# A transformer block on one core: position bias loaded as runs of 219 elements per query column and spread on GpSimd, and shift1/scale1 weights read from an array laid out by chunk

## The chip, the cores and the metric

The kernel runs on 1 core of one Trainium2 chip, in float32. The metric is the device time of one execution in microseconds (us). Three runs of the kernel before took 1788.45, 1788.52 and 1789.22 us; the median is 1788.52.

## The reference

One block of a diffusion transformer is computed for a sequence of 256 tokens (a grid of 4 rows by 64 columns) with 2048 features, beside a context of 256 tokens. Cut to what matters here:

```python
mod = split(silu(c) @ w_mod + b_mod, 6)          # shift1, scale1, gate1, shift2, scale2, gate2
h  = rms_norm(x, norm1_w) * (1 + sc1) + sh1      # hc: the same of ctx, with silu(c_ctx)
q, k, v, ft, pool, sv, sb, sc = split(h @ w_in)  # of hc only k and v
branches = (neighbourhood_attention(q, k, v, kc, vc, rpb), fourier, pooling, short convolution)
y = sum(sigmoid(h @ w_gate[i]) * (branches[i] @ w_branch[i]))
x = x + g1 * (y @ w_o)
x = x + g2 * ((silu(h2 @ w_ffn_gate) * (h2 @ w_ffn_up)) @ w_ffn_down)
```

In the attention each of 8 heads lets a query see, in each of the 4 rows, a window of 16 columns around its own column, and all of the context. To the score of a query in row r and column j with a key in row a and column c the bias `rpb[head, a - r + 7, c - j + 15]` is added; `rpb` has 15 x 31 numbers a head. Keys outside the window of columns are left out.

## The kernel before, in words

**Matrix products.** Each float32 weight tile (128 partitions x 1024, 512 KB) is loaded by the SP queue, rounded by ScalarE into a high part (line 90) and subtracted by VectorE into a low part (line 91), the *split*; TensorE then makes three products, high-high, high-low and low-high (lines 95 to 97). `gemm` does this for the large products, from five raw buffers (`NRAW`): `gt` is w_gate, `br` a branch weight, `wo` w_o, `fg`, `fu` and `dn` the three FFN weights. `in_groups` does the same for w_in, in six chunks of input features (`CHUNKS`, 1, 1, 2, 4, 4 and 4 tiles of 128 features); its sums are `in_x` for the tokens and `in_c` for the context.

**shift1 and scale1.** Before chunk i+1 is multiplied, `prep` makes its modulation and its normed input: `mod1(kt0, nk)` multiplies silu(c) and silu(c_ctx) by the columns of w_mod that belong to nk feature tiles, in four parts of four row tiles each. A part loads its rows of w_mod into tiles called `mod_w` (`mod_tile`, five buffers) and makes four matmuls of 32 columns (line 227, sums `mod_ps`); the fifth step, `finish`, transposes and sums them into modA and modB. `make_h` then transposes the normed tokens (`h_tpx`, `h_tpc`) and applies modA and modB. The steps of `prep` are dealt out between the tiles of the chunk before. Only the first chunk has nothing before it: `mod1(0, 1)` is the program's first work on TensorE. For chunks of one tile a `mod_w` tile has rows of 128 floats (512 bytes), for the others 256 floats (1 KB), always two loads a tile, one for shift and one for scale. The later four modulations (macc, line 405) are summed on VectorE from tiles called `mod`, paced by `pump`.

**Position bias.** Heads come in pairs (h0 = 0, 2, 4, 6). `bias_load(h0)` makes eight loads on GpSimd's own queue: for each head and each of the 4 grid rows of queries, 64 partitions (one a query column; queries stand in reversed column order, so that the source moves by one float from partition to partition) x 4 key rows x 64 floats. `bias_mask(h0)` adds the mask of columns, 0 or -1e30, on GpSimd (line 510). `scores` adds the result to the scores in PSUM on VectorE (line 550).

**Order.** The steps of the four heads' pairs, the norms of q and k and the other branches are functions in a list (`steps`), of which `gemm` and `in_groups` take one at a time; `Bi` are the bias loads, `Ma` the masks, `Sc` the scores. The framework places instructions on the engines by their dependencies and the program's order, and a tile whose buffer is free may be loaded earlier than its step stands. Each engine then works in order. A factor such as `rsh_q` (line 262, a power on GpSimd) belongs to the norm of q.

The few lines that set where the bias steps stand:

```python
steps += [Bi[0], Sq[0], Sq[1], Fa[0], Sq[2], Fa[1], Mu[0], Fa[2], Mu[1], Mu[2]]
steps += [Ma[0], Op[0], Bi[1], Sc[0], Sq[3], No[0], Op[1], Tu[0], Sc[1], Va[0], No[1], Fa[3], Tu[1], Ma[1]]
steps += [Bi[2], Mu[4], Fa[5], Va[3], Mu[5], Ma[2], Op[4], Bi[3], Sc[4], Op[5], No[4], Sc[5], Tu[4],
          No[5], Va[4], Ma[3], Op[6], Tu[5], Sc[6], ...]
```

Of the kernel before, what the change touches and what calls it, by code (L numbers as in the profile page):

```python
# [8 lines left out]
F32 = mybir.dt.float32  # L9
F32R = mybir.dt.float32r  # L10
AF = mybir.ActivationFunctionType
ALU = mybir.AluOpType
# [3 lines left out]
P = 128  # L16
D = 2048
S = 256
NT = S // P
KT = D // P  # L20
INW = 5632
FF = 5632
NH = 8
GRID_W = 64
ROWS = S // GRID_W
EPS = 1e-6
LOAD_AT = 8
# [8 lines left out]
CHUNKS = (1, 1, 2, 4, 4, 4)  # L36
# [6 lines left out]
def block_kernel(ctx: ExitStack, tc: tile.TileContext, t_in, out):  # L43
    nc = tc.nc
    x_d, ctx_d = t_in["x"], t_in["ctx"]
    w_mod, w_in = t_in["w_mod"], t_in["w_in"]
# [4 lines left out]
    sm = ctx.enter_context(tc.tile_pool(name="sm", bufs=1))  # L51
# [3 lines left out]
    def U(name, dtype=F32):  # L55
        return up.tile([P, 1024], dtype, tag="u", name=name, bufs=NU)

    def half(name, dtype=F32):
        return sm.tile([P, 512], dtype, tag="half", name=name, bufs=4)
# [4 lines left out]
    def tr_ps(name):  # L64
        return pst.tile([P, 512], F32, tag="tr", name=name)
# [5 lines left out]
    def mod_tile(name):  # L71
        return wp.tile([P, 1024], F32, tag="mraw", name=name, bufs=NMRAW)
# [132 lines left out]
    def mod1(kt0, nk):  # L205

        nf = nk * P
        box = {}

        def part(k0):  # L210
            if k0 == 0:
                box["ps"] = tr_ps(f"mod1_ps{kt0}")
            ps = box["ps"]
            kn = 2 if nk == 2 else 4
            rvs = []
            for ka in range(k0, k0 + 4, kn):
                raw = mod_tile(f"mod1_w{kt0}_{ka}")
                rv = raw.rearrange("p (k s f) -> p k s f", k=kn, s=2)
                for s_ in range(2):
                    nc.sync.dma_start(  # L220
                        rv[:, :, s_, :],
                        w_mod[ka * P:(ka + kn) * P, s_ * D + kt0 * P:s_ * D + kt0 * P + nf]
                        .rearrange("(k p) f -> p k f", p=P))
                rvs.append(rv)
            for j in range(4):
                kk = k0 + j
                nc.tensor.matmul(  # L227
                    ps[32 * j:32 * j + 32, :2 * nf],
                    lhsT=cst[:, kk, :],
                    rhs=rvs[j // kn][:, j % kn, :, :].rearrange("p s f -> p (s f)"),  # L230
                    start=k0 == 0, stop=k0 == KT - 4)

        def finish():
            ps = box["ps"]
            msb = half(f"msb{kt0}")
            nc.vector.tensor_copy(msb[:, :2 * nf], ps[:, :2 * nf])
            pt_ = tr_ps(f"mod1_t{kt0}")
            for i in range(2 * nk):
                nc.tensor.transpose(pt_[:, i * P:(i + 1) * P], msb[:, i * P:(i + 1) * P], ident)
            red = sm.tile([P, 2, nk, 2], F32, tag=f"red{nk}", name=f"red{kt0}", bufs=2)  # L240
            nc.vector.tensor_reduce(
                red.rearrange("p s k r -> p (s k) r"),
                pt_[:, :2 * nf].rearrange("p (i j r) -> p i r j", j=4, r=32)[:, :, 0:2, :],
                AX.X, ALU.add)
            for s_ in range(2):
                nc.vector.tensor_tensor(
                    red[:, s_], red[:, s_],
                    colB[:, s_ * KT + kt0:s_ * KT + kt0 + nk].unsqueeze(2).to_broadcast([P, nk, 2]),
                    ALU.add)
            nc.vector.tensor_copy(modB[:, kt0:kt0 + nk, :], red[:, 0])  # L250
            nc.vector.scalar_tensor_tensor(
                modA[:, kt0:kt0 + nk, :], red[:, 1], 1.0,
                colA[:, R_N1 + kt0:R_N1 + kt0 + nk].unsqueeze(2).to_broadcast([P, nk, 2]),
                ALU.add, ALU.mult)

        return [lambda k0=k0: part(k0) for k0 in range(0, KT, 4)] + [finish]


# [229 lines left out]
    rpb = t_in["rpb"]  # L488
    wmask = const.tile([P, GRID_W], F32, name="wmask")
    nc.gpsimd.dma_start(wmask, t_in["wmask"])  # L490

    biases = {}

    def bias_load(h0):


        b = U(f"bias{h0}").rearrange("p (h t f) -> p h t f", h=2, t=NT)
        for i in range(2):
            for r in range(ROWS):
                src = bass.AP(rpb.tensor, rpb.offset + (h0 + i) * 15 * 31 + (7 - r) * 31 - 48,  # L500
                              [[1, GRID_W], [31, ROWS], [1, GRID_W]])
                p0 = (r % 2) * GRID_W
                nc.gpsimd.dma_start(
                    b[p0:p0 + GRID_W, i, r // 2, :].rearrange("p (a c) -> p a c", a=ROWS), src)
            biases[h0 + i] = b[:, i]

    def bias_mask(h0):
        for h in (h0, h0 + 1):
            bv = biases[h].rearrange("p t (a c) -> p (t a) c", a=ROWS)
            nc.gpsimd.tensor_tensor(  # L510
                bv, bv, wmask.unsqueeze(1).to_broadcast([P, NT * ROWS, GRID_W]), ALU.add)

    def reverse(v):

# [246 lines left out]
    for i in range(1, len(CHUNKS) - 1):  # L761
        nk = CHUNKS[i]
# [12 lines left out]
    def last(g):  # L775
# [6 lines left out]
    Sq, Fa, Mu = zip(*[qk_norm(lambda st=st, g=g: st[g], n_) for n_, st, g in (  # L782
        ("q0", xin, 0), ("k0", xin, 2), ("c0", cin, 2), ("q1", xin, 1), ("k1", xin, 3), ("c1", cin, 3))])
    Bi, Ma = [[lambda f=f, h=h: f(h) for h in (0, 2, 4, 6)] for f in (bias_load, bias_mask)]

    def nop():
# [114 lines left out]
    for n in range(FF // 512):  # L901
# [11 lines left out]
        for pr in range(2):  # L913
            ps = tr_ps(f"m_tp{n}{pr}")
            for j in range(2):
                for t in range(NT):
                    b = pr * 2 + j
# [80 lines left out]
```

## Time and profile before

| What | Value |
|---|---|
| median of 3 runs | 1788.52 us |
| the profiled execution | 1794.19 us, its span 1792.4 us |
| TensorE busy | 1747.7 us (98%) |
| VectorE, ScalarE, GpSimd busy | 1132.5, 743.8 and 67.9 us |
| granted TensorE clock, mean | 0.992 |
| read from HBM | 400.58 MB, 225 GB/s over the span |

The span runs from the first to the last instruction of the profiled execution; all times of the trace are counted from its start. A busy TensorE is not TensorE at its peak: matmuls are pipelined and their ends modelled, and the granted clock says at what share of full speed they run. The DMA share of a stretch can pass 1, since packets overlap. SP, GpSimd and ScalarE issue loads to the same 16 DMA engines; "to landing" is the time from issue until the data is there.

### The profile page before, as it was taken

The page shows a single profiled execution, that of the slowest core. Times are in us where ns is not written, and L with a number is a line of the kernel's source. Part 1 is how long each engine was busy: PE and PEld are TensorE (multiplying, and loading weights), DVE is VectorE, ACT ScalarE, POOL GpSimd, SP SyncE. Part 2 cuts the span into 40 slices and gives each one's busy share as a digit, 9 for nine tenths or more (in the row PEclk, how much of TensorE's full clock was granted, in tenths as well). Part 3 has the DMA queues.
Part 4 walks back from the last instruction along what each step waited for, and adds up shares of the span by engine and source line. Part 5 has one row for each costly group of instructions (what it writes and reads, how often), then busy time and mean ns, then how long its engine had stood idle before and what let it go on. Part 6 is the DMA issues. An engine that isn't in the chain of part 4 may idle for free.

```text
span 1792.4 us, 21012 instructions
## 1 busy us (share of the span) xinstructions
PE 1747.7 (98%) x7874; PEld 1400.0 (78%) x7874; DVE 1132.5 (63%) x1294; ACT 743.8 (41%) x874; POOL 67.9 (4%) x90
## 2 busy tenths in 40 slices
PE   6998999999997999999999999999999999999998
PEld 3675777887886778888888878888888888888887
DVE  5874564775585876878787877775444444454544
ACT  5322232434553554444444454444444444433342
POOL 0001000031003000000000000000000000000000
PEclk9998999999999999999999999999999999999999
DMA  9788675565569768898999848886666666666663
GB/s 319 249 280 194 194 243 177 163 119 157 166 207 207 244 220 277 292 302 302 320 323 309 290 153 303 305 273 181 191 190 188 188 189 188 190 201 197 208 202 116
DMA packets 212874, 404.08 MB, mean 225 GB/s; under 512 B 14178, under 2 KB 53012, under 8 KB 212772
## 3 DMA queue, kind: packets, MB, share of 16 engines
q1 hardware_dynamic: 209732, 396.37, 68.7%
q0 software_dynamic: 1888, 4.26, 2.8%
q10 hardware_dynamic: 1152, 2.10, 0.3%
q8 instruction: 62, 1.02, 0.2%
q14 instruction: 40, 0.33, 0.1%
HBM read 400.58 MB, written 2.10 MB: 225 GB/s over the span
## 4 chain that ended last, share of the span: by engine, by line
PE 93%; DMA 4%; DVE 1%; issue 1%; SPq 1%; ACT 0%; POOL 0%; POOLq 0%; ACTq 0%; DVEq 0%
PE gt_ps L96 6%; PE gt_ps L97 6%; PE gt_ps L95 6%; PE in_psx L95 5%; PE fu_ps L95 4%; PE fu_ps L96 4%; PE fu_ps L97 4%; PE in_psx L96 4%; PE dn_ps L95 4%; PE dn_ps L97 4%; PE dn_ps L96 4%; PE fg_ps L95 4%; PE fg_ps L97 4%; PE fg_ps L96 4%; PE in_psx L97 4%; DMA gt_w<-in_w_gate 2%
## 5 line engine op out<-in xcount | busy, mean ns | idle before, releaser
L405 DVE SCALAR_TENSOR_TENSOR macc<-mod,cs,macc 128x1024 f32<-128x1024 f32 x128 | 163.3, 1278 | 0.0
L319 DVE TENSOR_TENSOR in_x<-in_x,in_psx 128x512 f32<-128x512 f32 x110 | 74.2, 683 | 47.3 <-PE in_psx L97 47.0
L90 ACT CAST in_2h<-in_w 128x1024 fp32r<-128x1024 f32 x33 | 34.8, 1054 | 165.0 <-PE in_psc L97 96.4
L90 ACT CAST in_0h<-in_w 128x1024 fp32r<-128x1024 f32 (+1 forms) x56 | 57.7, 1034 | 82.9 <-PE in_psc L97 27.0
L95 PE MATMUL in_psx<-in_0h,hxh 128*128 128x512 f32 x220 | 90.5, 418 | 1.3 <-ACT hxh L299 1.0
L96 PE MATMUL in_psx<-in_0l,hxh 128*128 128x512 f32 x220 | 87.8, 402 | 0.0
L97 PE MATMUL in_psx<-in_0h,hxl 128*128 128x512 f32 x220 | 86.4, 395 | 0.0
L91 DVE TENSOR_TENSOR in_0l<-in_w,in_0h 128x1024 fp32r<-128x1024 f32 (+1 forms) x56 | 67.1, 1199 | 10.7 <-ACT in_0h L90 10.7
L91 DVE TENSOR_TENSOR in_2l<-in_w,in_2h 128x1024 fp32r<-128x1024 f32 x33 | 40.4, 1224 | 40.1 <-ACT in_2h L90 40.1
L95 PEld LDWEIGHTS in_psx<-in_0h,hxh 128*128 128x128 f32 x220 | 41.8, 192 | 25.9 <-issue 8.6
L227 PE MATMUL mod_ps<-mod_w,cst 128*32 128x512 f32 (+1 forms) x288 | 46.1, 607 | 11.2 <-DMA mod_w<-in_w_mod 11.2
L96 PE MATMUL in_psx<-in_2l,hxh 128*128 128x512 f32 x132 | 51.8, 392 | 0.0
L95 PE MATMUL in_psx<-in_2h,hxh 128*128 128x512 f32 x132 | 51.5, 390 | 0.0
L97 PE MATMUL in_psx<-in_2h,hxl 128*128 128x512 f32 x132 | 51.5, 390 | 0.0
L96 PEld LDWEIGHTS in_psx<-in_0l,hxh 128*128 128x128 f32 x220 | 42.4, 193 | 10.8 <-issue 1.9
L97 PEld LDWEIGHTS in_psx<-in_0h,hxl 128*128 128x128 f32 x220 | 42.1, 191 | 9.1
L319 DVE TENSOR_TENSOR in_c<-in_c,in_psc 128x512 f32<-128x512 f32 x40 | 27.2, 684 | 28.6 <-PE in_psc L97 28.6
L227 PEld LDWEIGHTS mod_ps<-mod_w,cst 128*32 128x32 f32 x288 | 8.5, 114 | 34.1 <-issue 22.5
L95 PE MATMUL gt_ps<-gt_2h,hxh 128*128 128x512 f32 x64 | 26.6, 420 | 7.9 <-ACT gt_2h L90 7.9
L91 DVE TENSOR_TENSOR gt_2l<-gt_w,gt_2h 128x1024 fp32r<-128x1024 f32 x16 | 19.6, 1224 | 22.7 <-ACT gt_2h L90 22.7
L91 DVE TENSOR_TENSOR gt_12l<-gt_w,gt_12h 128x1024 fp32r<-128x1024 f32 x16 | 20.5, 1282 | 19.9 <-ACT gt_12h L90 19.8
L95 PE MATMUL in_psc<-in_0h,hch 128*128 128x512 f32 x80 | 31.5, 396 | 0.0
(657 smaller groups left out, 5184.4 us busy)
## 6 DMA issues: line engine op xcount, KB each, us to landing
mod<-in_w_mod SPq DMA_DIRECT2D x128, 512.0 KB, 5.5
gt_w<-in_w_gate SPq DMA_DIRECT2D x128, 512.0 KB, 5.5
fg_w<-in_w_ffn_gate SPq DMA_DIRECT2D x88, 512.0 KB, 4.2
fu_w<-in_w_ffn_up SPq DMA_DIRECT2D x88, 512.0 KB, 3.8
dn_w<-in_w_ffn_down SPq DMA_DIRECT2D x88, 512.0 KB, 4.8
in_w<-in_w_in SPq DMA_DIRECT2D x87, 512.0 KB, 5.5
mod_w<-in_w_mod SPq DMA_DIRECT2D x128, 256.0 KB, 5.6
wo_w<-in_w_o SPq DMA_DIRECT2D x32, 512.0 KB, 5.6
```

The costliest lines, as they stand in the source:

```text
L90: state["act"] = nc.scalar.copy(hv, src)
L91: state["dve"] = nc.vector.tensor_tensor(lv, src, hv.bitcast(F32), ALU.subtract)
L95: nc.tensor.matmul(ps, lhsT=xh, rhs=wh, start=first, stop=False)
L96: nc.tensor.matmul(ps, lhsT=xh, rhs=wl, start=False, stop=False)
L97: state["pe"] = nc.tensor.matmul(ps, lhsT=xl, rhs=wh, start=False, stop=last)
L227: nc.tensor.matmul(ps[32 * j:32 * j + 32, :2 * nf], lhsT=cst[:, kk, :], rhs=rvs[j // kn][:, j % kn, :, :].rearrange("p s f -> p (s f)"), s ...
L319: nc.vector.tensor_tensor(dst, dst, ps, ALU.add)
L405: nc.vector.scalar_tensor_tensor(macc[m][h_], mod_raw.pop((m, kk, h_)), cs[:, 0, kk:kk + 1], macc[m][h_], ALU.mult, ALU.add)
```

## The change

Two loads take another form. `bias_load` now loads a *window* for a pair of heads: for each half of the partitions (64 query columns, an even or an odd grid row) and each of the two heads one run of 219 floats (876 bytes), which holds all that the two query rows of that parity need. There is one buffer for it. `bias_mask` takes the bias tile and fills it from the window, with the mask added, by four additions on GpSimd: for each head and each half of the queries, 4 key rows at a step of 31 floats x 64 floats. And the host lays the first 4096 columns of w_mod out anew, `mod1`: for each `mod_w` tile a block of 128 partitions x 1024 floats in the order in which the tile holds them, so that one load with 4 KB a partition fills it.

```diff
+WIN = 5 * 31 + GRID_W
...
-            kn = 2 if nk == 2 else 4
+            kn = 4 // nk
...
-                rv = raw.rearrange("p (k s f) -> p k s f", k=kn, s=2)
-                for s_ in range(2):
-                    nc.sync.dma_start(
-                        rv[:, :, s_, :],
-                        w_mod[ka * P:(ka + kn) * P, s_ * D + kt0 * P:s_ * D + kt0 * P + nf]
-                        .rearrange("(k p) f -> p k f", p=P))
-                rvs.append(rv)
+                nc.sync.dma_start(raw, t_in["mod1"][kt0 * KT // 4 + ka * nk // 4])
+                rvs.append(raw.rearrange("p (k s f) -> p k s f", k=kn, s=2))
...
+    def window_load(h0):
+        w_ = sm.tile([P, 2, WIN], F32, tag="window", name=f"window{h0}", bufs=1)
+        for hf in range(2):
+            src = bass.AP(rpb.tensor, rpb.offset + h0 * 15 * 31 + (5 - hf) * 31 - 48,
+                          [[1, GRID_W], [15 * 31, 2], [1, WIN]])
+            nc.gpsimd.dma_start(w_[hf * GRID_W:(hf + 1) * GRID_W], src)
+        return w_
+
+    def bias_of(b, w_, i):
+        for t in range(NT):
+            v = w_[:, i, (1 - t) * 62:(1 - t) * 62 + GRID_W]
+            v = bass.AP(v.tensor, v.offset, [v.ap[0], [31, ROWS], [1, GRID_W]])
+            nc.gpsimd.tensor_tensor(b[:, i, t, :].rearrange("p (a c) -> p a c", a=ROWS), v,
+                                    wmask.unsqueeze(1).to_broadcast([P, ROWS, GRID_W]), ALU.add)
+        return b[:, i]
+
     def bias_load(h0):
-        b = U(f"bias{h0}").rearrange("p (h t f) -> p h t f", h=2, t=NT)
-        for i in range(2):
-            for r in range(ROWS):
-                src = bass.AP(rpb.tensor, rpb.offset + (h0 + i) * 15 * 31 + (7 - r) * 31 - 48,
-                              [[1, GRID_W], [31, ROWS], [1, GRID_W]])
-                p0 = (r % 2) * GRID_W
-                nc.gpsimd.dma_start(
-                    b[p0:p0 + GRID_W, i, r // 2, :].rearrange("p (a c) -> p a c", a=ROWS), src)
-            biases[h0 + i] = b[:, i]
+        windows[h0] = window_load(h0)
 
     def bias_mask(h0):
-        for h in (h0, h0 + 1):
-            bv = biases[h].rearrange("p t (a c) -> p (t a) c", a=ROWS)
-            nc.gpsimd.tensor_tensor(
-                bv, bv, wmask.unsqueeze(1).to_broadcast([P, NT * ROWS, GRID_W]), ALU.add)
+        b = U(f"bias{h0}").rearrange("p (h t f) -> p h t f", h=2, t=NT)
+        for i in range(2):
+            biases[h0 + i] = bias_of(b, windows[h0], i)
...
+    mod1 = []
+    w1 = a["w_mod"].reshape(D, 6 * D)[:, :2 * D].reshape(KT, P, 2, D)
+    for k0, nk in zip([sum(CHUNKS[:i]) for i in range(len(CHUNKS))], CHUNKS):
+        for k in range(k0, k0 + nk, 2):
+            n, f = 4 // min(2, nk), min(2, nk) * P
+            w_ = w1[:, :, :, k * P:k * P + f].reshape(KT // n, n, P, 2, f)
+            mod1.append(w_.transpose(0, 2, 1, 3, 4).reshape(KT // n, P, 1024))
+    arrays["mod1"] = np.concatenate(mod1, axis=0)
```

The order of TensorE's and ScalarE's instructions stays as it was; on VectorE one copy (colB) moves ahead of one scaling of x. On GpSimd and SP the order changes as follows.

GpSimd from the program's start, before (rs_x, rs_c are factors of the tokens' and the context's norm, rsh_q, rsh_k, rsh_c those of q and k; bias_2787 belongs to heads 0 and 1, bias_3038 to heads 2 and 3; in_x_307 is the gate of the short convolution):

```order
L490 DMA wmask<-in_wmask 128x64
L262 TENSOR_TENSOR rs_x<-ss_x_162,mhalf 128x1
L262 TENSOR_TENSOR rs_x<-ss_x_170,mhalf 128x1
L262 TENSOR_TENSOR rs_c<-ss_c_257,mhalf 128x1
L262 TENSOR_TENSOR rs_c<-ss_c_265,mhalf 128x1
L503 DMA bias_2787<-in_rpb 64x4x64 x8
L510 TENSOR_TENSOR bias_2787<-bias_2787,wmask 128x512 x2
L262 TENSOR_TENSOR rsh_q_2843<-ssh_q_2842,mhalf 128x8
L262 TENSOR_TENSOR rsh_k_2890<-ssh_k_2889,mhalf 128x8
```

The same place now (window_2723 and bias_2926 belong to heads 0 and 1, window_2971 to heads 2 and 3):

```order
L487 DMA wmask<-in_wmask 128x64
L498 DMA window_2723<-in_rpb 64x2x219 x2
L259 TENSOR_TENSOR rs_x<-ss_x_158,mhalf 128x1
L259 TENSOR_TENSOR rs_x<-ss_x_166,mhalf 128x1
L259 TENSOR_TENSOR rs_c<-ss_c_253,mhalf 128x1
L259 TENSOR_TENSOR rs_c<-ss_c_261,mhalf 128x1
L259 TENSOR_TENSOR rsh_q_2773<-ssh_q_2772,mhalf 128x8
L507 TENSOR_TENSOR bias_2926<-window_2723,wmask 128x256 x4
L498 DMA window_2971<-in_rpb 64x2x219 x2
L259 TENSOR_TENSOR rsh_k_2820<-ssh_k_2819,mhalf 128x8
```

The load for heads 0 and 1 has moved from behind the context's norm to the program's front, its masking behind the first factor of q, and the next pair's load follows that masking at once.

GpSimd in the middle of the program, from the second rsh_k on, before (bias_4320 belongs to heads 4 and 5, bias_4504 to heads 6 and 7; macc are the later modulations' sums):

```order
L262 TENSOR_TENSOR rsh_k_4216<-ssh_k_4215,mhalf 128x8
L503 DMA bias_4320<-in_rpb 64x4x64 x8
L510 TENSOR_TENSOR bias_4320<-bias_4320,wmask 128x512
L262 TENSOR_TENSOR rsh_c_4370<-ssh_c_4369,mhalf 128x8
L510 TENSOR_TENSOR bias_4320<-bias_4320,wmask 128x512
L503 DMA bias_4504<-in_rpb 64x4x64 x8
L510 TENSOR_TENSOR bias_4504<-bias_4504,wmask 128x512 x2
L388 MEMSET macc_0_5402 128x1024
```

The same place now (window_4250, for heads 4 and 5, was loaded further ahead, behind the masking of heads 2 and 3; window_4431 is for heads 6 and 7):

```order
L259 TENSOR_TENSOR rsh_k_4146<-ssh_k_4145,mhalf 128x8
L259 TENSOR_TENSOR rsh_c_4294<-ssh_c_4293,mhalf 128x8
L507 TENSOR_TENSOR bias_4371<-window_4250,wmask 128x256 x4
L498 DMA window_4431<-in_rpb 64x2x219 x2
L507 TENSOR_TENSOR bias_4668<-window_4431,wmask 128x256 x4
L385 MEMSET macc_0_5326 128x1024
```

Of sixteen loads between rsh_k and macc two are left, and both maskings stand behind rsh_c.

SP's queue at the start, before (x_tok are the tokens, packB a pack of small vectors, mod_w_0 to mod_w_12 the four tiles of the first `mod1`, in_w the first tiles of w_in):

```order
L167 DMA x_tok_81<-in_x 128x1024
L172 DMA packB<-in_packB 96x128
L220 DMA mod_w_0_117<-in_w_mod 128x4x128 x2
L220 DMA mod_w_4_124<-in_w_mod 128x4x128 x2
L220 DMA mod_w_8_131<-in_w_mod 128x4x128 x2
L220 DMA mod_w_12_138<-in_w_mod 128x4x128 x2
L333 DMA in_w_0_0_187<-in_w_in 128x1024
```

The same place now:

```order
L169 DMA x_tok_81<-in_x 128x1024
L174 DMA packB<-in_packB 96x128
L220 DMA mod_w_0_117<-in_mod 128x1024
L220 DMA mod_w_4_123<-in_mod 128x1024
L220 DMA mod_w_8_129<-in_mod 128x1024
L220 DMA mod_w_12_135<-in_mod 128x1024
L330 DMA in_w_0_0_183<-in_w_in 128x1024
```

Eight loads have become four, in the same place of the queue.

More of the change, by code (lines that the diff above doesn't have):

```diff
@@ L492, in block_kernel, with bias_mask @@
     biases = {}
+    def window_load(h0):
[12 more added lines that the diff above has]
+        return b[:, i]
+    windows = {}
     def bias_load(h0):
+        windows[h0] = window_load(h0)
+    def bias_mask(h0):
         b = U(f"bias{h0}").rearrange("p (h t f) -> p h t f", h=2, t=NT)
         for i in range(2):
-            for r in range(ROWS):
-                src = bass.AP(rpb.tensor, rpb.offset + (h0 + i) * 15 * 31 + (7 - r) * 31 - 48,
-                              [[1, GRID_W], [31, ROWS], [1, GRID_W]])
-                p0 = (r % 2) * GRID_W
-                nc.gpsimd.dma_start(
-                    b[p0:p0 + GRID_W, i, r // 2, :].rearrange("p (a c) -> p a c", a=ROWS), src)
-            biases[h0 + i] = b[:, i]
-    def bias_mask(h0):
-        for h in (h0, h0 + 1):
-            bv = biases[h].rearrange("p t (a c) -> p (t a) c", a=ROWS)
-            nc.gpsimd.tensor_tensor(
-                bv, bv, wmask.unsqueeze(1).to_broadcast([P, NT * ROWS, GRID_W]), ALU.add)
+            biases[h0 + i] = bias_of(b, windows[h0], i)
     def reverse(v):
```

## The prediction

> **What bounds the kernel now.** I read the page first, for the busiest engine.
>
> ```profile
> span 1792.4 us, 21012 instructions
> PE 1747.7 (98%) x7874; PEld 1400.0 (78%) x7874; DVE 1132.5 (63%) x1294; ACT 743.8 (41%) x874; POOL 67.9 (4%) x90
> ```
>
> TensorE (PE) idles 44.7 of 1792.4 us: whatever the change gains must come out of that, or out of time at a lower clock. So I cut the span into stages (columns: us, then busy time and count of PE, PEld, DVE, ACT and POOL, the granted clock, the DMA engines' share, GB/s).
>
> ```profile
> 0.00:12.50 12.50, 0.79 (x2) 0.37 (x2) 3.03 (x13) 7.39 (x11) 2.43 (x10) 1.00 0.83 250
> 12.50:50.00 37.50, 31.34 (x154) 19.45 (x154) 24.19 (x47) 20.14 (x33) 1.65 (x3) 0.95 1.02 333
> 80.00:90.00 10.00, 8.81 (x41) 3.50 (x40) 7.73 (x15) 2.19 (x3) 0.00 (x0) 1.00 0.80 267
> 150.00:167.00 17.00, 11.81 (x36) 5.04 (x35) 3.74 (x4) 2.10 (x2) 1.26 (x1) 0.70 1.00 292
> 250.00:262.00 12.00, 11.03 (x54) 6.78 (x51) 5.26 (x6) 2.10 (x2) 0.00 (x0) 1.00 0.99 308
> 375.00:400.00 25.00, 25.00 (x111) 20.06 (x110) 17.59 (x24) 9.68 (x13) 10.13 (x11) 1.00 0.71 103
> 500.00:537.00 37.00, 37.00 (x175) 30.06 (x174) 31.69 (x48) 19.79 (x32) 0.51 (x8) 1.00 0.63 201
> 557.00:574.00 17.00, 14.62 (x61) 11.56 (x60) 10.47 (x10) 6.71 (x8) 7.43 (x10) 0.90 1.00 228
> 574.00:592.00 18.00, 9.59 (x27) 6.39 (x26) 8.79 (x10) 6.21 (x7) 1.26 (x1) 0.72 0.72 238
> ```
>
> PE idles 17.9 us in the first 50, where the DMA engines are full; 5.2 from 150 to 167; 10.8 from 557 to 592; 1.2 from 80 to 90 and 1.0 from 250 to 262. The chain of waits names what ends the idle time (start, us, what).
>
> ```profile
> 12.72 5.33 DMA mod_w<-in_w_mod
> 18.19 1.12 PE mod_ps L227 x8
> ...
> 153.19 7.97 DMA mod_w<-in_w_mod
> ...
> 554.32 27.48 DMA gt_w<-in_w_gate
> ...
> 588.47 0.43 PE gt_ps L96
> ...
> 592.28 0.23 PE gt_ps L95
> ```
>
> Weights that land late, each time. One gate weight takes 27.48 us; the usual time is in the first line below (count, KB, median us to landing). After the wait matmuls step at 0.43 us before they are back at 0.23: the lower clock is part of the price. GpSimd's timeline shows what else was loading (start, us, what, and in brackets the wait before it).
>
> ```profile
> gt_w<-in_w_gate SPq DMA_DIRECT2D x128, 512.0 KB, 5.5
> bias<-in_rpb POOLq DMA_DIRECT2D x32, 64.0 KB, 9.0
> ```
>
> ```profile
> 137.83 4.92 POOL L503 DMA_DIRECT2D bias<-in_rpb  x8 [101.03 <-DVE in_x L319]
> 156.34 1.26 POOL L510 TENSOR_TENSOR bias<-bias,wmask 128x512 f32<-128x512 f32 x1 [7.72 <-DMA bias<-in_rpb]
> 359.15 1.67 POOL L262 TENSOR_TENSOR rsh_q<-ssh_q,mhalf 128x8 f32<-128x8 f32 x1 [201.56 <-DVE ssh_q L261]
> 370.07 1.64 POOL L262 TENSOR_TENSOR rsh_k<-ssh_k,mhalf 128x8 f32<-128x8 f32 x1 [9.25 <-DVE ssh_k L261]
> 377.96 4.92 POOL L503 DMA_DIRECT2D bias<-in_rpb  x8
> 538.79 5.01 POOL L503 DMA_DIRECT2D bias<-in_rpb  x8
> 560.79 4.93 POOL L503 DMA_DIRECT2D bias<-in_rpb  x8
> 581.85 1.26 POOL L510 TENSOR_TENSOR bias<-bias,wmask 128x512 f32<-128x512 f32 x1 [8.88 <-DMA bias<-in_rpb]
> ```
>
> Eight bias loads are under way from 138 to 156, and sixteen from 539 to 582, exactly over the two stalls; the late gate weight lands just when the last of them has (554.32 + 27.48 = 581.80). How they fill the DMA engines is shown by a stretch where they are alone (379 to 385), by two stretches of short and long rows without them, and by the shares of the queues from 541 to 556 (packets, MB, share of 16 engines; q0 is GpSimd's, q1 SP's).
>
> ```profile
> 379.00:385.00 6.00, 6.00 (x32) 5.02 (x31) 5.45 (x7) 2.11 (x2) 3.88 (x7) 1.00 0.99 37
> 12.00:16.00 4.00, 2.17 (x16) 0.46 (x16) 2.00 (x5) 0.00 (x0) 0.55 (x1) 1.00 1.22 291
> 27.00:30.00 3.00, 3.00 (x15) 2.38 (x14) 2.42 (x4) 1.58 (x4) 0.00 (x0) 1.00 1.03 411
> ```
>
> ```profile
> q0 software_dynamic: 231, 0.46, 56.7%
> q1 hardware_dynamic: 914, 2.02, 39.2%
> ```
>
> Alone they keep all 16 engines 99% busy at 37 GB/s. So one load of 65,536 bytes (256 runs of 256 bytes) costs 1.77 us of all engines and a set of eight 14.2 us; beside it the weights get what is left, 39%.
>
> **The bias part.** It removes 32 loads of 256 runs and adds 8 of 128 runs of 876 bytes: per pair of heads 256 runs and 224,256 bytes, where there were 2048 and 524,288. No run of 876 bytes is in the trace. Counted in runs, a pair costs 1.8 us of all engines; in bytes at 37 GB/s, 6.1. I take 2.5, near the price by runs: well-spread 512-byte rows go at 291 GB/s (12 to 16), so 37 is hardly a price of bytes. Both ends stay for the range.
>
> What it frees. From 150 to 167, 5.2 us of idle time; the half-speed time is 2 x 0.30 x 17 = 10.2 us, of which 5.0 are busy and 2.5 lost: 7.7. From 557 to 574, 2.4 idle and half of 3.4 us: 4.1. From 574 to 592, 8.4 idle, and 10.1 us at half speed of which PE works some 4.6, so 2.3: 10.7. Together 22.5. The first pair's load moves to the program's front, and each other pair is loaded as soon as the pair before it is masked, so that one load falls on the second stall in place of sixteen. There, five raw tiles of 512 KB at the 201 GB/s of 500 to 537 are 13 us of cover against 2.5 to 6.1; and from 375 to 400 a whole set of eight cost PE nothing (25.00 of 25.00), though at 103 GB/s. I leave 2.2 us standing, what the two stalls without any bias cost (1.2 and 1.0): -20.3.
>
> On GpSimd the masking of a pair becomes four additions of 256 elements for two of 512.
>
> ```profile
> L510 POOL TENSOR_TENSOR bias<-bias,wmask 128x512 f32<-128x512 f32 x8 | 11.1, 1392 | 49.8 <-DMA bias<-in_rpb 49.8
> 390.58 1.72 PE s_ps L546 x4
> ```
>
> At 1392 ns for 512, one of 256 costs 0.7 to 1.4 us and a pair 2.8 to 5.6, on an engine that is 4% busy. The first mask now stands behind the factor at 359.15 (1.67 us), is done by 367, and the scores that need it start at 390.58: 23 us of cover, so nothing. Behind those additions GpSimd queues the next window's load and the factor of 370.07, which they let through in time. Without that cover the addition of scores and bias would hold VectorE, and the splits queued behind it, for up to 5.6 us.
>
> **The shift1 and scale1 part.** 128 loads of 256 KB become 64 of 512 KB, with 4 KB a partition in place of rows of 512 bytes (the first two chunks) or 1 KB.
>
> ```profile
> L220 SPq DMA_DIRECT2D mod_w<-in_w_mod x128: 367/460/2876, 3.7 to 284.9; - x128
> 20.29 0.63 PE L297 MATMUL h_tpx<-ident,x_tok 128*128 128x128 f32 x2
> ```
>
> 512-byte rows go at 291 GB/s (12 to 16), 4 KB rows at 411 (27 to 30). The first matmuls wait for the first eight loads, 2.10 MB: 7.2 us become 5.1, so -2.1. But the first window pair is now read there too, where the engines are full, and takes its price from the same engines: +2.5 (1.8 to 6.1). The start comes out at +0.4 (-0.3 to +4.0). The second chunk frees as much of the queue again ahead of the context's tokens, but their norm follows on ScalarE behind work of the first chunk, so I count none of it; at most some 4 us of the idle time there go too.
>
> Later PE catches up with its five tiles, from 80 to 90 and from 250 to 262. One issue of 460 ns goes and the rows get faster, the time to landing stays: -1.0 of 2.2 (0 to -2.2). SP is freed of 64 x 0.46 = 29 us of issuing, which is on no path. VectorE now copies colB ahead of the first scaling of x, which has until the transposes at 20.29: nothing.
>
> **A rule weighed.** Whether the relayout pays at the start hangs on those two rates, 291 and 411. The Trainium skill, "DMA: Bandwidth & Descriptors" (Specifications), calls 512 bytes enough for line rate; by it the -2.1 and the -1.0 would be nothing and the sum 3.1 us higher. This trace disagrees, 291 against 411 GB/s.
>
> **The sum.** -20.3 + 0.4 - 1.0 = -20.9. The profiled execution took 1794.19 us (the span and 1.8 around it): 1773.3. The median of the runs shown is 1788.52, 5.7 lower; with the same difference I predict 1767.6 us.
>
> **Rivals.**
> 1. *VectorE takes over.* Its 19.26 us of work from 557 to 592 would stand in 20.2 once 14.8 are gone. If half of the 14.8 stays as waits for its splits: 1775. Against it: it is busy 31.69 of 37 us from 500 to 537, and PE is full there.
> 2. *Bytes are the price of the windows.* A pair costs 6.1 us, the start +4.0, the rest as forecast: 1771. For it: every load reads the same 1860 bytes a head. Against it: the 291 GB/s of other short rows.
> 3. *Rows of 512 bytes are fast enough*, and the 291 GB/s have another cause: +3.1, so 1771. The page above says so; the two rates speak against it.
> 4. *The bias loads are not what stalls.* They would pass at the 291 GB/s of other short rows, 1.8 us a set; the stalls, the weights' own, stay, and -2.1 + 0.8 - 1.0 leaves 1786. Against it: 99% busy at 37 GB/s, and 56.7% beside 39.2%. (The same page of the Trainium skill, in the section on the GpSimd path, fits a load as 2 us plus its bytes at 436 GB/s; that is this rival's case, and the row at 37 GB/s disagrees.)
> 5. *Slower: the front chokes.* If runs of 876 bytes at unaligned addresses are cut into pieces that each cost as much as a run, the first pair holds up the start, where PE has nothing else to do. Pieces of 64 bytes are 14 x 256 = 3584, 24.8 us of all engines, the start +22.7: there it has eaten the gain. Pieces of 32 bytes: start +47, and the pair on the second stall stops PE as now: 1788.5 + 47 - 6.7 - 1 = 1828. For it: no such run in the trace. Against it: runs of 256 bytes would be cut already, and cost 7 ns each over 16 engines.
>
> **Chances.** Forecast 0.63; rivals 0.14, 0.10, 0.05, 0.04, 0.04 in their order. Faster by over 0.2% (3.6 us, about what a measurement of this kernel can tell): 0.63 + 0.14 + 0.10 + 0.05 = 0.92; same 0.04; slower 0.04. The range: all of 22.5 and 2.2, the start's -0.3 and the 4 us behind it give 1759; rival 1, if besides most of the 5.7 us by which the profiled execution is longer belongs to these stalls, 1779.
>
> **What would show it.** Right: from 150 to 167 no idle time and clock 1.00, and the same over the stretch that was 557 to 592; no gate weight over 12 us to landing; about 400 GB/s where the first mod_w tiles load; a window landing 4 to 8 us after its issue. Wrong: a window load over 10 us; the first mod_ps matmuls' last group, at 18.19 now, later than 21; idle time over 3 us before 600 that a bias, a split or a gate weight ends.

## The result and the profile after

| | before | after |
|---|---|---|
| median, us (4 runs each) | 1788.80 (1788.45 to 1789.22) | 1764.93 (1763.79 to 1765.30) |
| profiled execution | 1794.19 | 1765.03 |
| its span | 1792.4 | 1763.1 |
| ratio of the times, 95% interval | | 0.9865 (0.9848 to 0.9882) |

Forecast were 1767.6 us in a range from 1759 to 1779. The median fell by 23.9 us, the span by 29.3: the profiled execution of before lies 5.4 us above this median, that of after on it. That gap is a result of its own, below.

The page of after, its busy times:

```profile
PE 1736.6 (98%) x7874; PEld 1395.8 (79%) x7874; DVE 1132.1 (64%) x1294; ACT 744.2 (42%) x874; POOL 56.9 (3%) x74
```

Of the span of 1763.1 us TensorE idles 26.5, not 44.7. The stretches of the prediction again, with the same columns (the instructions of 557 to 592 now stand some 14 to 29 us earlier, so that place is taken in one row from 537 to 580):

```profile
12.00:16.00 4.00, 2.77 (x21) 0.64 (x24) 3.03 (x7) 0.75 (x2) 0.55 (x1) 1.00 1.02 409
80.00:90.00 10.00, 8.80 (x42) 3.88 (x41) 7.71 (x13) 1.82 (x3) 0.00 (x0) 1.00 0.75 270
150.00:167.00 17.00, 17.00 (x88) 11.87 (x87) 8.80 (x14) 3.97 (x4) 0.00 (x0) 1.00 0.77 282
250.00:262.00 12.00, 12.00 (x59) 9.13 (x58) 5.01 (x11) 2.10 (x2) 0.00 (x0) 1.00 0.80 291
537.00:580.00 43.00, 43.00 (x194) 34.41 (x194) 37.41 (x44) 23.45 (x33) 12.35 (x11) 1.00 0.86 276
```

Both large stalls are gone, idle time and low clock alike; so is the small one at 250, while that at 80 stands (1.20 idle, 1.19 before). No gate weight took more than 7.4 us to land, where one took 27.48. From 12 to 16 us, where the first modulation weights load, 291 GB/s have become 409. Among the 55 longest pieces of the chain of waits up to 620 us only three are waits for a weight (start, us, what); the two groups of matmuls serve as milestones below:

```profile
5.44 11.41 DMA mod_w<-in_mod
...
82.17 3.64 DMA mod_w<-in_mod
...
117.37 3.84 DMA mod_w<-in_mod
...
176.59 1.85 PE mod_ps L224 x16
...
269.88 1.85 PE mod_ps L224 x16
```

GpSimd's timeline of after (the loads of the windows, the additions that spread them, and three events that before has too):

```profile
2.45 1.24 POOL L498 DMA_DIRECT2D window<-in_rpb  x2
...
35.37 0.55 POOL L259 TENSOR_TENSOR rs_c<-ss_c,mhalf 128x1 f32<-128x1 f32 x1 [2.86 <-DVE ss_c L258]
345.56 1.65 POOL L259 TENSOR_TENSOR rsh_q<-ssh_q,mhalf 128x8 f32<-128x8 f32 x1 [309.64 <-DVE ssh_q L258]
347.18 2.64 POOL L507 TENSOR_TENSOR bias<-window,wmask 128x256 f32<-128x256 f32 x4
...
541.00 6.32 POOL L507 TENSOR_TENSOR bias<-window,wmask 128x256 f32<-128x256 f32 x4
...
611.54 0.96 POOL L385 MEMSET macc<- 128x1024 f32 x1 [46.69 <-PE p_ps L577]
```

Four additions take 2.64 us right behind the first factor, where 2.8 to 5.6 were forecast; those of the third pair take 6.32, more than that. TensorE has no idle time around either, so they cost nothing, as forecast. Where the time came from is read off by following the same instruction through both traces. Before has them here, in GpSimd's timeline and in the chain of waits:

```profile
36.26 0.55 POOL L262 TENSOR_TENSOR rs_c<-ss_c,mhalf 128x1 f32<-128x1 f32 x1 [2.85 <-DVE ss_c L261]
...
641.03 0.95 POOL L388 MEMSET macc<- 128x1024 f32 x1 [57.92 <-ACT br_0h L90]
```

```profile
188.03 1.85 PE mod_ps L227 x16
...
283.48 1.85 PE mod_ps L227 x16
```

The difference at each milestone, less that at the one ahead of it, is what the stretch between them gained: -0.9 up to the context's norm at 36 us; -10.6 up to 188 (the first stall); -2.2 up to 283 (the small stall at 250); -15.9 up to 641 (the second stall). The sum, -29.5, is the whole difference of the spans (29.3).

### The profile page after: what moved, and what is told of

Same layout as the page of the kernel before. It is cut to its first block, busy times and chain, and to the rows that moved or that the text cites. A ratio compares the mean times of both kernels' runs of the same rounds, so it can differ in the third digit from the quotient of the medians.

```text
span 1763.1 us, 20830 instructions
## 1 busy us (share of the span) xinstructions
PE 1736.6 (98%) x7874; PEld 1395.8 (79%) x7874; DVE 1132.1 (64%) x1294; ACT 744.2 (42%) x874; POOL 56.9 (3%) x74
## 4 chain that ended last, share of the span: by engine, by line
PE 96%; DMA 1%; DVE 1%; issue 1%; ACT 0%; SPq 0%; POOL 0%; POOLq 0%; DVEq 0%; ACTq 0%
PE gt_ps L98 7%; PE gt_ps L99 7%; PE gt_ps L97 7%; PE in_psx L97 5%; PE in_psx L98 5%; PE fu_ps L97 5%; PE fu_ps L99 5%; PE fu_ps L98 5%; PE in_psx L99 5%; PE dn_ps L98 5%; PE dn_ps L99 5%; PE dn_ps L97 4%; PE fg_ps L97 4%; PE fg_ps L99 4%; PE fg_ps L98 4%; PE br_ps L97 2%
## 5 line engine op out<-in xcount | busy, mean ns | idle before, releaser
L224 PE MATMUL mod_ps<-mod_w,cst 128*32 128x512 f32 (+1 forms) x288 | 40.8, 593 | 3.0 <-DMA mod_w<-in_mod 2.9
L98 PE MATMUL in_psc<-in_0l,hch 128*128 128x512 f32 x80 | 31.2, 390 | 0.0
L99 PE MATMUL in_psc<-in_0h,hcl 128*128 128x512 f32 x80 | 31.1, 389 | 0.0
L98 PEld LDWEIGHTS in_psx<-in_2l,hxh 128*128 128x128 f32 x132 | 24.8, 188 | 6.0 <-DVE hcl L299 0.8
```

The lines of the kernel that those rows point to most:

```text
L98: nc.tensor.matmul(ps, lhsT=xh, rhs=wl, start=False, stop=False)
L99: state["pe"] = nc.tensor.matmul(ps, lhsT=xl, rhs=wh, start=False, stop=last)
L224: nc.tensor.matmul(ps[32 * j:32 * j + 32, :2 * nf], lhsT=cst[:, kk, :], rhs=rvs[j // kn][:, j % kn, :, :].rearrange("p s f -> p (s f)"), s ...
```

## The experiments

Theory after the result: the bias loads are what stalls TensorE, the relayout of shift1 and scale1 gives some 2 us, and the window at the start costs less than forecast. Rivals: the relayout did more than its share; rows of 512 bytes are fast enough; and of the old loads' price, that it goes by runs (the prediction), by bytes, or by the addresses that they read. No kernel here leaves anything out of the computation; some add loads that nothing uses.

| kernel | median, us | ratio to before, 95% interval |
|---|---|---|
| bias alone | 1767.12 (1766.99 to 1767.68) | 0.9876 (0.9862 to 0.9889) |
| shift1 and scale1 alone | 1787.84 (1786.45 to 1790.94) | 0.9992 (0.9983 to 1.0001) |
| after, first window later | 1763.32 (1762.92 to 1764.25) | 0.9855 (0.9841 to 0.9868) |
| after, five windows in front | 1772.59 (1772.33 to 1772.76) | 0.9906 (0.9891 to 0.9921) |
| after, last pair's bias as before | 1764.58 (1763.38 to 1764.87) | 0.9860 (0.9846 to 0.9873) |
| before, the same loads far apart | 1765.64 (1764.65 to 1766.53) | 0.9867 (0.9851 to 0.9884) |
| later window and six tiles | 1761.48 (1760.45 to 1762.48) | 0.9846 (0.9833 to 0.9860) |

The kernel before ran beside them at medians of 1789.49, 1788.97 and 1788.81 us.

**Each part alone.** The bias alone keeps the loads of the kernel before in `mod1`:

```diff
-            kn = 4 // nk
+            kn = 2 if nk == 2 else 4
...
-                nc.sync.dma_start(raw, t_in["mod1"][kt0 * KT // 4 + ka * nk // 4])
-                rvs.append(raw.rearrange("p (k s f) -> p k s f", k=kn, s=2))
+                rv = raw.rearrange("p (k s f) -> p k s f", k=kn, s=2)
+                for s_ in range(2):
+                    nc.sync.dma_start(rv[:, :, s_, :], w_mod[...])
+                rvs.append(rv)
```

> The changed bias with shift1 and scale1 loaded as before (128 loads in rows of 512 bytes and 1 KB). Before stands at 1788.8 us, after at 1764.9. The forecast's own terms for this part alone, -20.3 and +2.5 for the window at the start, give 1771.0. Theory A, the two stalls cost more than was counted and the window at the start less: the whole of 22.5 goes, the window costs about 1, so 1767.3. Theory B, the 3 us by which the change did better than forecast come from the relayout: 1771. Rival 3, rows of 512 bytes are fast enough and the relayout gives nothing: 1764.9, as after. Trace: by all of them no idle time from 150 to 167 at a clock of 1.00.

The other part alone is the kernel before with the new `mod1`.

> The changed shift1 and scale1 loads with the bias loaded as before. The forecast's terms (-2.1 at the start, -1.0 at the small stalls) give 1785.7. Theory A: 1786.2 (-2.1 at the start, 0.5 later). Theory B, the relayout frees more of the DMA engines and shortens the bias stalls too: some 6 us, 1782.8. Rival 3: 1788.8, no change. Trace: by A and the forecast the last of the first modulation matmuls ends about 2.1 us earlier, and the stalls over the eight bias loads and the sixteen stay as in before.

Measured 1767.12 and 1787.84. The bias is worth 22.4 us by itself, the relayout 1.7, or 2.2 on top of the bias (1767.12 to 1764.93); together 24.1, nearly what both do at once (23.9). Theory A fits the first number. The second lies between its 1786.2 and rival 3's 1788.8, beside a before that ran 0.7 higher than those count from; theory B would have had 1771 and 1782.8, rival 3 1764.9 and no change. The interval of the relayout alone reaches to no change. What it gives is told by 1767.12 against 1764.93, whose runs lie 1.7 us apart at the least, and by the traces. The same milestones, of the bias alone and then of shift1 and scale1 alone, in GpSimd's timeline and in the chain of waits:

```profile
36.86 0.55 POOL L264 TENSOR_TENSOR rs_c<-ss_c,mhalf 128x1 f32<-128x1 f32 x1 [2.86 <-DVE ss_c L263]
...
614.38 0.96 POOL L390 MEMSET macc<- 128x1024 f32 x1 [46.69 <-PE p_ps L582]
```

```profile
178.82 1.85 PE mod_ps L229 x16
...
272.75 1.85 PE mod_ps L229 x16
```

```profile
34.31 0.55 POOL L257 TENSOR_TENSOR rs_c<-ss_c,mhalf 128x1 f32<-128x1 f32 x1 [2.86 <-DVE ss_c L256]
...
636.00 0.96 POOL L383 MEMSET macc<- 128x1024 f32 x1 [58.39 <-ACT br_0h L90]
```

```profile
186.40 1.85 PE mod_ps L222 x16
...
279.77 1.85 PE mod_ps L222 x16
```

By stretch, against before: the bias alone +0.6, -9.8, -1.5, -15.9; the relayout alone -2.0, +0.3, -2.1, -1.3. The two large stalls go with the bias. At the start the relayout saves 2.0, of which 0.9 are left with the window beside it. The small stall at 250 shrinks with either part. It does so as well in a kernel below in which only the addresses of the bias loads change, in its chain of waits -1.5 from 188 to 283:

```profile
177.67 1.85 PE mod_ps L227 x16
...
271.59 1.85 PE mod_ps L227 x16
```

No bias load of before is under way within 90 us of that stall, so it may belong to the one execution that was profiled there; no run tells.

**What a window costs at the start.** Once it is held back, once there are five.

```diff
         w_ = sm.tile([P, 2, WIN], F32, tag="window", name=f"window{h0}", bufs=1)
+        if h0 == 0:
+            nc.gpsimd.tensor_copy(w_[:, 0, 0:1], modA[:, 1, 1:2])
```

> The changed kernel with the first window load held back: a GpSimd copy of one value of the second chunk's scale into the window stands ahead of the load, so that it starts near 49 us and no longer at 2.4. The price of the window pair at the start comes back: by the forecast's 2.5 us 1762.4; by runs (1.8) 1763.1; by bytes (6.1) 1758.8; by the shift of the landings seen in the trace of after (about 0.9) 1764.0; if the load hides wholly, 1764.9. At 49 us the DMA engines have room (59 to 77%), so it costs nothing there.

```diff
     load_tokens("x", x_d)
+    for n in range(4):
+        more = half(f"more{n}")[:, :2 * WIN].rearrange("p (i f) -> p i f", i=2)
+        for hf in range(2):
+            src = bass.AP(..., [[1, GRID_W], [15 * 31, 2], [1, WIN]])
+            nc.gpsimd.dma_start(more[hf * GRID_W:(hf + 1) * GRID_W], src)
```

> The changed kernel with four more copies of the first window pair loaded at the program's front, into buffers that nothing reads then: the suspected price five times. By the forecast's 2.5 us a pair +10: 1774.9; by runs (1.8) +7.2: 1772.1; by bytes at 37 GB/s (6.1) +24.4: 1789.3; by the 0.9 seen in the landings +3.6: 1768.5. Rival 5, runs cut into pieces that each cost as much as a run, 22 us and more a pair: above 1850.

One pair less gives 1.6 us, four more cost 7.7, or 1.9 each. The 7.7 are clear of the spread; the 1.6 are less certain, since the slowest run with the later window (1764.25) lies above the fastest of after (1763.79). The price by runs (1.8) fits, that by bytes (6.1) and rival 5's do not; the forecast's 2.5 was too much, and the 0.9 read from the landings too little.

**Half of the second stall's loads.** Heads 6 and 7 alone get eight loads in the old form, where the kernel before had sixteen (`bias_load` and `bias_mask` of before, for `h0 == 6` only).

> The changed kernel with the bias of the last two heads alone loaded as before: eight loads of 256 runs in place of two windows, where before had sixteen. After stands at 1764.9. Cover theory (the prediction's arithmetic): beside the weights a set of eight takes some 25 us, the weights get 39% or some 155 GB/s of the 201 they ask, 1.2 MB short, 5.7 us, under the 13 us that five raw tiles cover: no stall, 1765 to 1766. Proportional theory, every load takes its price from TensorE: half of the 15.8 us that the sixteen cost, 7.9, so 1772.8.

Measured 1764.58: nothing, as the cover theory says. That place of this kernel, and the shares of the queues from 541 to 556 (packets, MB, share of 16 engines):

```profile
545.00:564.00 19.00, 19.00 (x88) 15.11 (x87) 16.25 (x19) 10.51 (x17) 8.47 (x11) 1.00 1.00 215
```

```profile
q1 hardware_dynamic: 1089, 2.59, 53.8%
q0 software_dynamic: 209, 0.45, 46.0%
```

The DMA engines are full and the eight loads take 46% of them from 541 to 556, but TensorE works all 19 us. What is loaded ahead was cover enough for eight such loads and not for sixteen: a stall is not the sum of its loads' prices. That holds for this place. At the first stall eight loads alone cost some 10 us, and no run changed the number of raw tiles, so that these set the limit is argued and not shown.

**Loads by themselves.** Behind the last output sets of eight loads run alone, one set after the other, in one execution of each kernel. The first of three such kernels:

```diff
+    probe("hot", [[1, 64], [31, 4], [1, 64]], 256, lambda l: (rpb, ...))
+    probe("apart", [[W, 64], [3072, 4], [1, 64]], 256, lambda l: (w_mod, l * 64))
+    probe("odd", [[W, 64], [3072, 4], [1, 64]], 256, lambda l: (w_mod, l * 128 + 17))
+    probe("same", [[0, 64], [128, 4], [1, 64]], 256, lambda l: (w_mod, l * 512))
+    probe("win", [[1, 64], [465, 2], [1, WIN]], 512, lambda l: (rpb, ...))
+    probe("wapart", [[W, 64], [3072, 2], [1, WIN]], 512, lambda l: (w_mod, l * 256))
```

> The changed kernel, and behind its last output sets of eight GpSimd loads each by itself, with nothing else on the DMA engines: a first set to warm up; 256-byte runs as the old bias had them (sliding by 4 bytes from partition to partition); 256-byte runs at addresses far apart and aligned; the same far apart and at odd addresses; 256-byte runs of the same aligned addresses on every partition; windows of 876 bytes as now; 876-byte runs far apart. Each set is 512 KB in 2048 runs, or 449 KB in 1024. Forecast, the price goes by runs: some 14 us for every set of 256-byte runs and half of it, 7, for both sets of 876-byte runs. Rival 2, bytes of the same few addresses are the price: 14 for the sliding and the same addresses, some 12 for the windows, but far apart 1.8 to 5 (the eight issues of 0.6 us). If unaligned addresses are the price: sliding and odd slow, aligned fast. Rival 4, the loads are no slower than other short rows: 5 for all of them.

The stretches of the sets "hot" (the old bias's), "apart", "same" and "win" (the last two columns are the DMA engines' share and GB/s), and the loads' median us from issue to landing:

```profile
1766.00:1779.00 13.00, 0.00 (x0) 0.00 (x0) 0.00 (x0) 0.00 (x0) 4.93 (x9) 0.50 0.68 40
1779.50:1787.00 7.50, 0.00 (x0) 0.00 (x0) 0.00 (x0) 0.00 (x0) 5.19 (x10) 0.50 0.27 70
...
1794.70:1802.50 7.80, 0.00 (x0) 0.00 (x0) 0.00 (x0) 0.00 (x0) 4.96 (x9) 0.50 0.24 67
1803.00:1810.50 7.50, 0.00 (x0) 0.00 (x0) 0.00 (x0) 0.00 (x0) 5.03 (x11) 0.50 0.51 120
```

```profile
pbhot<-in_rpb POOLq DMA_DIRECT2D x8, 64.0 KB, 7.5
pbapart<-in_w_mod POOLq DMA_DIRECT2D x8, 64.0 KB, 2.3
```

The old loads hold all engines for 0.68 x 13 = 8.8 us a set (not the forecast's 14.2, which went by the first 6 us of a set), the same runs far apart for 2.0, a quarter. So the price by runs falls: 256 runs need not cost 1.8 us, 0.25 will do. Every partition reading the same aligned places ("same", 2.9 us to landing) is nearly as fast, so it is no price of few addresses as such, and odd addresses cost nothing ("odd" takes 2.3 as well). The Trainium skill, "DMA: Bandwidth & Descriptors" (the section on the GpSimd path), fits a load as 2 us plus its bytes at 436 GB/s, an estimate of 2.15 for 64 KB: the far-apart loads agree with 2.3, the old ones do not, with 7.5.

**The same loads, far apart, in the kernel.** This is the test of that in place: the kernel before, whose bias loads keep their number, queue, time, runs and bytes, and read a copy in which each run has 256 bytes of its own.

```diff
-                src = bass.AP(rpb.tensor, rpb.offset + (h0 + i) * 15 * 31 + (7 - r) * 31 - 48,
-                              [[1, GRID_W], [31, ROWS], [1, GRID_W]])
+                src = t_in["rpb_far"][h0 + i, r].rearrange("a p c -> p a c")
```

> The kernel before with its 32 bias loads unchanged in number, place, runs (256 of 256 bytes each) and bytes, but read from a copy of the position bias laid out so that every run has an address of its own, 256 bytes from its neighbour; shift1 and scale1 as before. The forecast's theory, a load's price goes by its runs: no change, 1789. New theory, from the sets measured alone (68% of all engines over 13 us for the sliding runs, 27% over 7.5 us for the same runs far apart): the overlapping addresses are the price, so both stalls vanish as with the windows; the window kernel with the old shift1 and scale1 loads stands at 1767.1 and pays some 1.8 us for a load at the start that this one does not have: 1765 to 1766.

Measured 1765.64: 1.5 us below the bias part alone, which pays for a window at the start, and with none of its edits. Its queues from 541 to 556, and a load's us to landing:

```profile
q1 hardware_dynamic: 1894, 4.39, 89.2%
q0 software_dynamic: 220, 0.46, 14.4%
```

```profile
bias<-in_rpb_far POOLq DMA_DIRECT2D x32, 64.0 KB, 4.2
```

Nearly as many packets and as many bytes of the bias as before (231 and 0.46 MB there) take 14.4% and not 56.7%, and the weights get 4.39 MB, not 2.02. What stalled TensorE was where the loads read.

**How narrow is too narrow.** Two more kernels vary the steps of a load's runs, each load in a region of its own:

> As the first measurement of load sets alone, eight loads of 256 runs of 256 bytes in each set: a set to warm up; the old bias's runs again (a step of 4 bytes from partition to partition, of 124 bytes from run to run, all eight loads in some 2.8 KB); the step of 4 bytes with runs 512 bytes apart; the step of 124 bytes with every partition at the same place; the old steps with each load in a region of its own; steps of 64 and 128 bytes, aligned; and the step of 124 bytes with the partitions far apart. The old set took 12.9 us from its first issue to its last landing, far-apart runs 6.9. If the overlap of one partition's own runs (124 bytes) is the price, sets four, five and seven are slow, three fast. If the step of 4 bytes between partitions is, three and five are slow, four and seven fast. If it is that all eight loads read the same 2.8 KB, set five is fast and only the old one slow. If unaligned overlap is, the aligned set is fast and three to five slow.

> As the two measurements of load sets alone, eight loads of 256 runs of 256 bytes in each set, each load in a region of its own. Every partition at the same place with steps of 124 bytes from run to run (slow before: 13.4 us from the first issue to the last landing); the same with steps of 128 bytes, aligned; with steps of 128 bytes from an odd address; with steps of 260 bytes, so that a partition's runs do not overlap; and steps of 4 bytes from partition to partition with runs 128 and 260 bytes apart. If what costs is that runs start at unaligned places, all but the second are slow (over 10 us). If it is overlap, the first three and the fifth are slow and those of 260 bytes fast (7 us). If both are needed, the first, third and fifth are slow. If only the step of 124 bytes is, the first alone.

Some rows of the second kernel and of the third (median us to landing; the views leave digits out of names, so that "odd" is here a set with 124 bytes from run to run, not that of the first kernel):

```profile
pbslide<-in_w_mod POOLq DMA_DIRECT2D x8, 64.0 KB, 2.6
pblap<-in_w_mod POOLq DMA_DIRECT2D x8, 64.0 KB, 7.3
pbhotal<-in_w_mod POOLq DMA_DIRECT2D x8, 64.0 KB, 2.4
pbodd<-in_w_mod POOLq DMA_DIRECT2D x8, 64.0 KB, 2.3
```

```profile
pbevenlap<-in_w_mod POOLq DMA_DIRECT2D x8, 64.0 KB, 6.7
pbstep<-in_w_mod POOLq DMA_DIRECT2D x8, 64.0 KB, 4.8
```

Set against the stretch of addresses from which one load reads (63 steps between partitions, three between runs, and 256 bytes), with the other sets of these two kernels and two of the first ("hot" and "same"; "hot" and "lap" ran twice):

| set | step between partitions, runs (bytes) | stretch (bytes) | us to landing |
|---|---|---|---|
| lap, evenlap, oddlap | 0, 124 or 128 | 628 to 640 | 7.3 and 7.5, 6.7, 9.6 |
| hot, hotfar, slidelap | 4, 124 or 128 | 880 to 892 | 7.5 and 7.5, 8.1, 8.3 |
| step, slidestep | 0 or 4, 260 | 1036 to 1288 | 4.8, 4.7 |
| same, slide | 0 or 4, 512 | 1792 to 2044 | 2.9, 2.6 |
| hotal | 64, 128 | 4672 | 2.4 |
| odd | far apart, 124 | large | 2.3 |

No guess holds alone: the aligned set with steps of 128 bytes is slow, the overlap of one partition's runs alone is not ("odd"), and runs of 260 bytes' step, which don't overlap, are half slow. What orders the sets is how narrow a stretch a whole load reads from: slow under 900 bytes, half slow from 1.0 to 1.3 KB, nearly as fast as any from 1.8 KB on. It is not how often a byte is read (64 times in "same" and in "step", which took 2.9 and 4.8 us). In these sets a narrower stretch also means fewer separate blocks of memory, and nothing here tells the two apart; what in the memory or the engines does this was not tried.

**A version that beats both.** The later window, and six tiles for the modulation weights:

```diff
-NMRAW = 5
+NMRAW = 6
...
-NU = 34
+NU = 33
```

> The kernel with the later first window, with six tiles in place of five for the modulation weights (and 33 of the large buffers in place of 34): for a version better than both. The stall that is left near 82 us (some 1.9 us of lost time) waits for a modulation weight whose tile came free late; if a sixth tile takes it away, 1763.3 falls to 1761.5. If the loads are late because the DMA engines are full, or for want of the 34th buffer: 1763.3 or more.

Measured 1761.48, 3.45 below after. The size is as expected, the place is not, so the match is luck. The chain of waits with the later window and five tiles, then with six:

```profile
79.94 3.79 DMA mod_w<-in_mod
...
115.29 3.65 DMA mod_w<-in_mod
```

```profile
79.59 3.50 DMA mod_w<-in_mod
...
113.64 2.71 PE mod_ps L224 x24
```

The wait at 80 us stays, that at 115 is gone.

## Why the prediction was right, and where not

- *Bias loads stall TensorE; without them both stalls go.* Right, shown by the bias alone and by the same loads far apart. Rival 4 had this wrong, and rival 1 too: no wait for a split came in the stalls' place.
- *First stall 7.7.* The mechanism right, the size too small: -9.8 with the bias alone. The failed term is the half-clock loss of 2.5, reckoned as half of 5.0 us of "busy" time, as if a matmul there took twice its time. In the prediction's own stretch sixteen `mod_ps` matmuls begin at 151.70 and the next matmul comes at 163.14:

```profile
151.70 1.05 PE L227 MATMUL mod_ps<-mod_w,cst 128*32 128x512 f32 x4
157.01 3.35 PE L227 MATMUL mod_ps<-mod_w,cst 128*32 128x512 f32 x8 [4.26 <-DMA mod_w<-in_w_mod]
161.29 1.92 PE L227 MATMUL mod_ps<-mod_w,cst 128*32 128x512 f32 x4 [0.93 <-DMA mod_w<-in_w_mod]
163.14 0.80 PE L95 MATMUL in_psx<-in_0h,hxh 128*128 128x512 f32 x1
```

  In after the same sixteen run in one go:

```profile
150.98 1.92 PE L224 MATMUL mod_ps<-mod_w,cst 128*32 128x512 f32 x16
152.83 0.50 PE L97 MATMUL in_psx<-in_0h,hxh 128*128 128x512 f32 x1
```

  11.44 us for what takes 1.85: 9.6 lost in this group, of which the idle column shows 5.2. They count as 6.3 us busy, for 1.9 us of work: the eight from 157.01 take 0.42 us each at a granted clock of 0.50, in after 0.12, so more than the clock held them; what else did is not shown.
- *Second stall 14.8, and 2.2 of both stalls stay.* It gave 15.9 and nothing stays. The window pair there (7.4% of the DMA engines from 541 to 556) is covered by what is loaded ahead; eight of the old loads were covered too.
- *The start, +0.4.* -0.9. The relayout's -2.1 held (-2.0 alone, 409 GB/s where 411 was assumed), against rival 3. The Trainium skill, "DMA: Bandwidth & Descriptors" (Specifications), calls 512 bytes enough for line rate; the traces disagree, 291 against 409 GB/s. The window's 2.5 was the mis-sized term, 1.6 to 1.9 by two experiments. Its lower end, by runs, was the right number for a wrong reason: with addresses far apart a run costs a seventh of that (0.25 us for 256).
- *Small stalls, -1.0 of 2.2.* The one at 250 went whole (-2.2), the one at 80 stays. As the one at 250 shrinks without the relayout too, the reason given for it is not shown.
- *The price of the old loads goes by runs.* The step that failed as a reason. Rival 2 had noticed that every load reads the same few bytes and took it for a price of bytes; it is one of addresses. The size was off as well: 1.77 us a load went by the first 0.22 of a set's 0.52 MB; alone a set holds the engines for 8.8 us, 1.1 a load. Neither changes this forecast much, since the windows spread a load over 3 KB (two runs of 876 bytes, 1860 apart, and 252 of sliding), but an engineer who believed it would have cut runs where a copy with spread addresses was enough.
- *The same difference of 5.7 between profiled execution and median.* It failed: 5.4 in before, 0.1 in after. The terms lacked even more, since they sum to -20.9 and the trace has -29.3. The two errors cancel but for 2.7 us: that 1767.6 lies so near is in part luck. Of the excess little is placed. Before ran from 1788.09 to 1791.14 beside the first experiments (one run of 2192 left out), the relayout alone from 1786.45 to 1790.94; the kernels without both large stalls spread by 0.4 to 2.0, over fewer runs, and their profiled executions lie within 1.2 of the median. That fits stalls of a length that changes from run to run, but it is not shown. The relayout alone, profiled at 1789.39, has the first stall 0.3 longer and the stretch of the second 1.3 shorter than before; the small stall at 250 may be another 2.

## What to carry to other kernels

When a transfer is slow for its bytes, look at the addresses before counting runs: here a broadcast or sliding read whose whole load comes from under some 1.3 KB took two to four times as long to land as the same runs spread out, and a spread copy in memory repaired it without touching the schedule. A stall beside full DMA engines need not shrink in proportion to its cause: here half of sixteen loads cost nothing, likely because of the tiles that are loaded ahead. Take the loss of a stall from the distance between the same instructions in two places or kernels, not from the idle column: matmuls that creep along after it count as busy.

## What was not expected of the hardware

- 64 KB in 256 runs of 256 bytes, alone on the engines, landed after 2.3 us from far-apart addresses and after 6.7 to 9.6 us from under 900 bytes; alignment made no difference in the fast case (2.3 both), and in the narrow one 6.7 against 9.6.
- Rows of 512 bytes of the modulation weights moved at 291 GB/s in before and 290 with the bias alone, and 4 KB a partition at 409; the time that this gave at the start was 2.0 us.
- A window pair occupies the engines for 0.51 x 7.5 / 4 = 1.0 us alone, and costs the start 1.6 to 1.9 us of time beside full queues. In the traces the last group of the first modulation begins 1.0 us later with it (16.90 us in after, 15.87 with the later window); where the rest arises stays open.
